# Attention's running maxima, its biases on ScalarE and its weight sums from a column of ones in a two-layer hybrid backbone

## The chip, the cores and the metric

One core of one Trainium2 chip runs the whole program. The metric is the device time of one execution in microseconds; the time before is 4437.48 us, the median of three runs (4432.41 to 4437.69). The kernel is written with a tile framework: it lays out the buffers, adds the semaphores, and orders each engine's instructions by priority with a timeline of its own at build time. On the chip each engine then works its queue in that fixed order.

## The reference

Two layers, each over 2048 latent tokens (which also read 512 cached context tokens) and 256 prompt tokens. One input projection feeds four parallel branches (latent attention, Hyena long convolution, S5 state space, chunked GLA); each is gated, and one output projection joins them. The change touches the attention alone:

```python
def one(qi):                                   # 128 queries, 4 heads
    s = jnp.einsum('bqhd,bkhd->bhqk', qi, k).astype(jnp.float32) * (MLA_QK ** -0.5)
    pr = jax.nn.softmax(s, axis=-1).astype(v.dtype)
    return jnp.einsum('bhqk,bkhd->bqhd', pr, v)
...
o_mla = block_attention(q, jnp.concatenate([k_ctx.astype(k.dtype), k], axis=1),
                        jnp.concatenate([v_ctx.astype(v.dtype), v], axis=1))
```

A latent query sees 512 + 2048 = 2560 keys, a prompt query 256. A head has 96 query and key columns and 64 value columns.

## The kernel before

Per layer there are 4 heads by 18 query tiles of 128 (16 latent, 2 prompt): 72 units, 144 in all. `mla_prep` (L307) projects queries, keys and values, splits each into an fp16 high part and an fp16 remainder, and stores them in DRAM; L415 and L416 write the value's two halves side by side, high part in columns 0 to 63 of `vd`. `load` in `attention` (L459) brings one head's keys and values into SBUF, two heads at a time (`bufs=2`).

A latent unit goes through three key chunks, of 1024, 1024 and 512. `scores` (L473) makes each chunk: for each part of 512 keys three matmuls into one PSUM bank (L485 to L487) and a maximum over it on VectorE (DVE, L488); for a chunk of two parts the larger of both (L492); the bias `nb`, which is minus the scaled maximum plus a constant (L493); then for each part the exponential on ScalarE (ACT, L495), which also gives the sum of the weights through `accum_out`, read by an instruction of its own that has the same line. `values` (L499) makes the fp16 high part of the weights on ACT, or in one of three cases on DVE (L508, L510), their remainder on POOL (L511), has both transposed by a DMA from SyncE's queue (L513), and multiplies with the values on TensorE (L517, L518) into one third of the bank `om`. Only one such bank exists, and the transposes that `emit` (L1951) makes share it. `combine` (L520) joins the three chunks: the smallest bias (L528), the chunks' factors (L529, ACT), the weighted sums and their reciprocal (L530 to L533), the three thirds of `om` with their factors (L536, L538) and the two halves of the columns (L540). The scores of the next chunk are issued before the values of this one, so `combine` comes after the first scores of the next unit.

The scores have three PSUM banks (`pss`), in the last part of layer 1 two more. The order around the attention is set by priority streams: GLA first, attention of heads 0 and 1 next, then Hyena, then attention of heads 2 and 3 with the output projection. These run interleaved, from about 1100 to 2440 us in layer 0 and from about 3330 us to the end in layer 1.

```python
mc = m[:, 2 * c:2 * c + 1]
if len(sps) > 1:
    nc.vector.tensor_tensor(out=mc, in0=mc, in1=m[:, 2 * c + 1:2 * c + 2], op=ALU.max)
nc.vector.tensor_scalar(out=nb[:, c:c + 1], in0=mc, scalar1=nssc, scalar2=LN2_15, op0=ALU.mult, op1=ALU.add)
for i, d in enumerate(sps):
    nc.scalar.activation(e[:, i * 512:min(i * 512 + 512, n)], d, AF.Exp, bias=nb[:, c:c + 1], scale=ssc,
                         accum_out=su[:, 2 * c + i:2 * c + i + 1])
```

Of the kernel before, what the change touches and what calls it, by code (L numbers as in the profile page):

```python
# [8 lines left out]
F32 = mybir.dt.float32  # L9
# [297 lines left out]
def mla_prep(s, l, p, tp, pp):  # L307
# [67 lines left out]
    for t in range(22):  # L375
# [39 lines left out]
        nc.scalar.activation(vd[:, :, 0:64], kv[:, :, 64:128], AF.Copy, scale=sv)  # L415
        nc.vector.scalar_tensor_tensor(out=vd[:, :, 64:128], in0=kv[:, :, 64:128], scalar=sv, in1=vd[:, :, 0:64],  # L416
# [38 lines left out]
def attention(s, l, units, tp, kp, bank, ps_o, emit):  # L455
# [3 lines left out]
    def load(h):  # L459

        out = []
        for a, b, nm in ((0, PAST + LAT, ""), (PAST + LAT, PAST + LAT + PR, "p")):
            K = kp.tile([128, 2, b - a], F16, tag="KT" + nm, name="KT" + nm)
            V = kp.tile([128, (b - a) // 128, 128], F16, tag="V" + nm, name="V" + nm)
            nc.sync.dma_start(K, s.KT[l][:, h, :, a:b])
            nc.sync.dma_start(V, s.V[l][h, :, a // 128:b // 128])
            out.append((K, V))
        return out
# [4 lines left out]
    def scores(u, c, k0, n):  # L473

        KT = u["KT"]
        e = tp.tile([128, 1024], F32, tag="e", name="e", bufs=3)[:, 0:n]
        nb, su, m = u["nb"], u["su"], u["m"]
        parts = range(0, n, 512)
        sps = []
        for i, a in enumerate(parts):  # L480
            w = min(512, n - a)
            d = bank(u["h"], u["t"])[:, 0:w]
            kh, kl = [KT[:, j, k0 + a:k0 + a + w] for j in range(2)]
            qh, ql = [u["qt"][:, j] for j in range(2)]
            nc.tensor.matmul(d, lhsT=qh, rhs=kh, start=True, stop=False)  # L485
            nc.tensor.matmul(d, lhsT=qh, rhs=kl, start=False, stop=False)  # L486
            nc.tensor.matmul(d, lhsT=ql, rhs=kh, start=False, stop=True)  # L487
            nc.vector.tensor_reduce(m[:, 2 * c + i:2 * c + i + 1], d, axis=AX.X, op=ALU.max)  # L488
            sps.append(d)
        mc = m[:, 2 * c:2 * c + 1]  # L490
        if len(sps) > 1:
            nc.vector.tensor_tensor(out=mc, in0=mc, in1=m[:, 2 * c + 1:2 * c + 2], op=ALU.max)  # L492
        nc.vector.tensor_scalar(out=nb[:, c:c + 1], in0=mc, scalar1=nssc, scalar2=LN2_15, op0=ALU.mult, op1=ALU.add)  # L493
        for i, d in enumerate(sps):
            nc.scalar.activation(e[:, i * 512:min(i * 512 + 512, n)], d, AF.Exp, bias=nb[:, c:c + 1], scale=ssc,  # L495
                                 accum_out=su[:, 2 * c + i:2 * c + i + 1])
        u["e"][c] = e

    def values(u, c, k0, n, first):  # L499

        e, V = u["e"].pop(c), u["V"]
        if first:
            u["om"] = ps_o.tile([128, 3, 128], F32, tag="om", name="om")
# [11 lines left out]
        for i in range(nk):  # L515
            v = V[:, k0 // 128 + i]
            nc.tensor.matmul(om[:, c], lhsT=pt[:, i], rhs=v, start=i == 0, stop=False)  # L517
            nc.tensor.matmul(om[:, c, 0:64], lhsT=pt[:, nk + i], rhs=v[:, 0:64], start=False, stop=i == nk - 1)  # L518

    def combine(u, C):  # L520
        nb, su, om = u["nb"], u["su"], u["om"]
        al, dn, mx = small(4, "al"), small(1, "dn"), small(1, "mx")
        w = tp.tile([128, 128], F32, tag="wo", name="wo")
        sc = su.rearrange("p (c i) -> p c i", i=2)
        last = C - 1
        if C > 1:

            nc.vector.tensor_reduce(mx, nb[:, 0:C], axis=AX.X, op=ALU.min)  # L528
            nc.scalar.activation(al[:, 0:C], nb[:, 0:C], AF.Exp, bias=mx, scale=-1.0)  # L529
            nc.vector.tensor_tensor(out=sc[:, 0:C], in0=sc[:, 0:C], in1=al[:, 0:C].unsqueeze(2).to_broadcast([128, C, 2]), op=ALU.mult)  # L530
            nc.vector.tensor_reduce(dn, su[:, 0:u["ns"]], axis=AX.X, op=ALU.add)
            nc.vector.reciprocal(dn, dn)
            nc.vector.tensor_scalar(out=al[:, 0:C], in0=al[:, 0:C], scalar1=dn, scalar2=None, op0=ALU.mult)  # L533
        else:
            nc.vector.reciprocal(al[:, 0:1], su[:, 0:1])
        nc.vector.tensor_scalar(out=w, in0=om[:, last], scalar1=al[:, last:C], scalar2=None, op0=ALU.mult)  # L536
        for c in range(last):
            nc.vector.scalar_tensor_tensor(out=w, in0=om[:, c], scalar=al[:, c:c + 1], in1=w, op0=ALU.mult, op1=ALU.add)  # L538
        o = pairs[u["h"] // 2, u["t"]][1]
        nc.vector.tensor_tensor(out=o[:, u["h"] % 2 * 64:u["h"] % 2 * 64 + 64], in0=w[:, 0:64], in1=w[:, 64:128], op=ALU.add)  # L540
# [16 lines left out]
    for h, t in units:  # L557
        if h not in kv:
            kv[h] = load(h)
        if (h // 2, t) not in pairs:  # L560
# [6 lines left out]
        u = dict(h=h, t=t, qt=pairs[h // 2, t][0][:, h % 2], KT=KT, V=V, e={}, m=small(8, "m"), nb=small(4, "nb"), su=small(8, "su"),  # L567
                 ns=5 if t < 16 else 1)
        if C > 1:
            nc.vector.memset(u["su"][:, 5:6], 0.0)  # L570
# [1264 lines left out]

PADF = 640


def body(tc, I, O, depth=DEPTH):
# [21 lines left out]
    with ExitStack() as top:  # L1861
# [5 lines left out]
        for l in range(depth):  # L1867
# [73 lines left out]
            kp = att.enter_context(pool(name=f"kv{l}", bufs=2, side="right"))  # L1941
            ps_s = att.enter_context(pool(name=f"pss{l}", bufs=3, space=PSUM))
# [89 lines left out]
```

## Time and profile before

| | |
|---|---|
| median of 3 runs | 4437.48 us |
| the profiled execution's own time | 4438.93 us |
| its span, first to last instruction | 4436.9 us |
| mean granted TensorE clock | 0.897 of full speed |
| TensorE matmul busy | 3680.0 us (83%) |
| VectorE (DVE) busy | 3222.7 us (73%) |
| ScalarE (ACT) busy | 2175.1 us (49%) |
| GpSimd (POOL) busy | 2048.8 us (46%) |
| DMA queue, share of 16 engines | 71.8% |

Busy time is a union of the instructions' spans. A view of stretches gives it for one stretch of the span; a view of lines gives groups of instructions by source line, with total, mean, and what ended the engine's idle time before them; a view of one line gives shortest, median and longest. The chain is followed back from the last instruction, at each step to what released it, so time on it is time that the end depended on; here it reaches back to about 3145 us.

### The profile page before, as it was taken

How to read it: one execution, taken by the hardware profiler on the slowest of the kernel's cores; microseconds unless marked ns; L12 is line 12 of the kernel's file. 1: busy time of each engine (PE TensorE's matmuls, PEld its weight loads, DVE VectorE, ACT ScalarE, POOL GpSimd, SP SyncE). 2: the span in 40 equal slices, each digit the busy share in tenths (PEclk: the TensorE clock that was granted, in tenths of full speed). 3: DMA queues.
4: the chain of work that ended last, by engine and by line, in shares of the span. 5: the costliest groups of instructions: out<-in, count | busy, mean ns of one | idle time of the engine just before them, and what ended most of it. 6: DMA issues, size and time to landing. Idle time of an engine off the chain costs nothing. (4 is left out here: it accounts for less than half of the span.)

```text
span 4436.9 us, 67211 instructions
## 1 busy us (share of the span) xinstructions
PE 3680.0 (83%) x21852; PEld 2141.3 (48%) x21852; DVE 3222.7 (73%) x8340; ACT 2175.1 (49%) x4333; POOL 2048.8 (46%) x2025
## 2 busy tenths in 40 slices
PE   6899889787877887769887688889998888667898
PEld 2644545343555555424443554545565555434444
DVE  4775589984788887776786678866548887767774
ACT  3533334556545564675453344363435555545563
POOL 2553354741555654654453244424325555434553
PEclk7999999898777887989998899999998888887999
DMA  7746657656776788998988565633448776999886
GB/s 207 193 122 182 175 146 191 188 155 221 168 172 150 173 186 212 239 235 203 250 192 203 148 156 145 154 111 123 145 156 193 184 168 157 210 246 240 173 185 157
DMA packets 1343430, 799.91 MB, mean 180 GB/s; under 512 B 989588, under 2 KB 1221296, under 8 KB 1341544
## 3 DMA queue, kind: packets, MB, share of 16 engines
q1 hardware_dynamic: 1343080, 795.63, 71.8%
q8 instruction: 173, 2.83, 0.3%
q14 instruction: 177, 1.45, 0.1%
HBM read 352.12 MB, written 207.37 MB: 126 GB/s over the span
## 5 line engine op out<-in xcount | busy, mean ns | idle before, releaser
L511 POOL TENSOR_TENSOR ph<-e,ph 128x1024 f16<-128x1024 f32 (+2 forms) x400 | 725.5, 1821 | 650.4 <-ACT ph L508 323.9
L495 ACT ACTIVATE e<-sp,nb,ssc 128x512 f32<-128x512 f32 (+1 forms) x656 | 499.9, 767 | 415.7 <-DVE nb L493 347.0
L488 DVE TENSOR_REDUCE m<-sp 128x1 f32<-128x512 f32 (+1 forms) x656 | 438.0, 676 | 172.0 <-PE sp L487 170.2
L268 PE MATMUL mm<-hT,ws 128*128 128x512 f16 (+1 forms) x1440 | 526.5, 366 | 26.2 <-DVE wqh L75 13.3
L269 PE MATMUL mm<-hT,ws 128*128 128x512 f16 (+1 forms) x1440 | 526.4, 366 | 0.0
L270 PE MATMUL mm<-hT,ws 128*128 128x512 f16 (+1 forms) x1440 | 525.8, 365 | 0.0
L517 PE MATMUL om<-V,pt 128*128 128x128 f16 x2560 | 303.8, 235 | 132.1 <-DMA pt<-ph 90.6
L485 PE MATMUL sp<-KT,qt 128*128 128x512 f16 x640 | 271.5, 424 | 102.5 <-ACT e L495 99.1
L517 PEld LDWEIGHTS <-pt 128*128 128x128 f16 x2592 | 258.9, 109 | 171.6 <-DMA pt<-ph 125.1
L508 ACT CAST ph<-e 128x1024 f16<-128x1024 f32 (+2 forms) x268 | 269.0, 1004 | 117.3 <-DMA pt<-ph 115.2
L518 PE MATMUL om<-V,pt 128*128 128x64 f16 x2560 | 293.7, 206 | 0.0
L518 PEld LDWEIGHTS <-pt 128*128 128x128 f16 x2592 | 248.2, 105 | 71.6 <-issue 58.5
L486 PE MATMUL sp<-KT,qt 128*128 128x512 f16 x640 | 271.4, 424 | 0.0
L487 PE MATMUL sp<-KT,qt 128*128 128x512 f16 x640 | 268.9, 420 | 0.0
L1606 PE MATMUL lv<-qh,kh 32*128 32x128 f32 x1440 | 227.7, 324 | 25.1 <-DVE m L492 10.2
L1606 PEld LDWEIGHTS lv<-qh,kh 32*128 32x128 f32 x1440 | 188.0, 218 | 98.8 <-issue 30.3
L1817 PE MATMUL mm<-wo,bh 128*128 128x512 f16 x576 | 223.7, 389 | 7.7 <-DVE oy L1820 6.7
L268 PE MATMUL mm<-ws,hT 128*128 128x256 f16 (+1 forms) x864 | 215.4, 264 | 15.8 <-ACT z L1688 13.4
L269 PEld LDWEIGHTS <-ws 128*128 128x128 f16 x1440 | 143.8, 100 | 175.2 <-issue 49.4
L1818 PE MATMUL mm<-wo,bh 128*128 128x512 f16 x576 | 224.1, 389 | 4.2 <-DVE wo L1772 4.2
L1819 PE MATMUL mm<-wo,bh 128*128 128x512 f16 x576 | 223.9, 389 | 2.8 <-DVE bh L1792 2.8
L268 PEld LDWEIGHTS <-ws 128*128 128x128 f16 x1440 | 143.9, 100 | 150.9 <-issue 26.1
(522 smaller groups left out, 9489.1 us busy)
## 6 DMA issues: line engine op xcount, KB each, us to landing
kab<-KS SPq DMA_DIRECT2D x128, 256.0 KB
wf<-in_w_in SPq DMA_DIRECT2D x22, 1024.0 KB
b<-br SPq DMA_DIRECT2D x36, 512.0 KB
A1F<-a SPq DMA_DIRECT2D x64, 256.0 KB
zg<-z SPq DMA_DIRECT2D x64, 256.0 KB
b<-A1F SPq DMA_DIRECT2D x32, 512.0 KB
KS<-k SPq DMA_DIRECT2D x64, 256.0 KB
aw<-in_ada_w SPq DMA_DIRECT2D x64, 256.0 KB
```

What stands on the lines that cost most here:

```text
L268: nc.tensor.matmul(ps, lhsT=lh, rhs=rh, start=i == 0, stop=False)
L269: nc.tensor.matmul(ps, lhsT=lh, rhs=rl, start=False, stop=False)
L270: nc.tensor.matmul(ps, lhsT=ll, rhs=rh, start=False, stop=i == n - 1)
L485: nc.tensor.matmul(d, lhsT=qh, rhs=kh, start=True, stop=False)
L486: nc.tensor.matmul(d, lhsT=qh, rhs=kl, start=False, stop=False)
L488: nc.vector.tensor_reduce(m[:, 2 * c + i:2 * c + i + 1], d, axis=AX.X, op=ALU.max)
L495: nc.scalar.activation(e[:, i * 512:min(i * 512 + 512, n)], d, AF.Exp, bias=nb[:, c:c + 1], scale=ssc, accum_out=su[:, 2 * c + i:2 * c + i ...
L508: nc.scalar.copy(ph[:, 0:n], e)
L511: nc.gpsimd.tensor_tensor(out=ph[:, n:2 * n], in0=e, in1=ph[:, 0:n], op=ALU.subtract)
L517: nc.tensor.matmul(om[:, c], lhsT=pt[:, i], rhs=v, start=i == 0, stop=False)
L518: nc.tensor.matmul(om[:, c, 0:64], lhsT=pt[:, nk + i], rhs=v[:, 0:64], start=False, stop=i == nk - 1)
L1606: nc.tensor.matmul(ps[:, cc], lhsT=kh[hh, cc], rhs=qh[hh, cc], start=True, stop=True, tile_position=(32 * h, 0))
```

## The change

Values: the two halves of the value columns change places, remainder first, high part in columns 64 to 127. A 129th column of ones is set in SBUF by POOL, so the tile's rows are 130 wide and the load fills 128 of them. The first value matmul takes 129 columns and the second takes 65 in place of 64, so that column 128 of `om` is the sum of the weights.

Scores: the maximum of a chunk is taken over all parts so far (one `tensor_reduce` per chunk), so it runs up; the bias is made on ACT; the exponentials no longer give sums.

Combine: the last chunk's factor is one, the other two come from the difference of biases; the first third of `om` is scaled on ACT, the second added on DVE with its factor, the third added on DVE; then the reciprocal of column 128, one half of the columns scaled on ACT, and the last instruction on DVE. The tiles `su`, `al`, `dn` and `mx` go. A pad of 192 bytes a partition is added.

```diff
-        nc.scalar.activation(vd[:, :, 0:64], kv[:, :, 64:128], AF.Copy, scale=sv)
-        nc.vector.scalar_tensor_tensor(out=vd[:, :, 64:128], in0=kv[:, :, 64:128], scalar=sv, in1=vd[:, :, 0:64],
+        nc.scalar.activation(vd[:, :, 64:128], kv[:, :, 64:128], AF.Copy, scale=sv)
+        nc.vector.scalar_tensor_tensor(out=vd[:, :, 0:64], in0=kv[:, :, 64:128], scalar=sv, in1=vd[:, :, 64:128],
...
-            V = kp.tile([128, (b - a) // 128, 128], F16, tag="V" + nm, name="V" + nm)
+            V = kp.tile([128, (b - a) // 128, 130], F16, tag="V" + nm, name="V" + nm)
             nc.sync.dma_start(K, s.KT[l][:, h, :, a:b])
-            nc.sync.dma_start(V, s.V[l][h, :, a // 128:b // 128])
+            nc.gpsimd.memset(V[:, :, 128:129], 1.0)
+            nc.sync.dma_start(V[:, :, 0:128], s.V[l][h, :, a // 128:b // 128])
...
-        mc = m[:, 2 * c:2 * c + 1]
-        if len(sps) > 1:
-            nc.vector.tensor_tensor(out=mc, in0=mc, in1=m[:, 2 * c + 1:2 * c + 2], op=ALU.max)
-        nc.vector.tensor_scalar(out=nb[:, c:c + 1], in0=mc, scalar1=nssc, scalar2=LN2_15, op0=ALU.mult, op1=ALU.add)
+        mc, k = m[:, 0:1], 2 * c + len(sps)
+        if k > 1:
+            mc = m[:, 5 + c:6 + c]
+            nc.vector.tensor_reduce(mc, m[:, 0:k], axis=AX.X, op=ALU.max)
+        nc.scalar.activation(nb[:, c:c + 1], mc, AF.Copy, scale=nssc, bias=LN2_15)
         for i, d in enumerate(sps):
-            nc.scalar.activation(e[:, i * 512:min(i * 512 + 512, n)], d, AF.Exp, bias=nb[:, c:c + 1], scale=ssc,
-                                 accum_out=su[:, 2 * c + i:2 * c + i + 1])
+            nc.scalar.activation(e[:, i * 512:min(i * 512 + 512, n)], d, AF.Exp, bias=nb[:, c:c + 1], scale=ssc)
...
-            nc.tensor.matmul(om[:, c], lhsT=pt[:, i], rhs=v, start=i == 0, stop=False)
-            nc.tensor.matmul(om[:, c, 0:64], lhsT=pt[:, nk + i], rhs=v[:, 0:64], start=False, stop=i == nk - 1)
+            nc.tensor.matmul(om[:, c], lhsT=pt[:, i], rhs=v[:, 0:129], start=i == 0, stop=False)
+            nc.tensor.matmul(om[:, c, 64:129], lhsT=pt[:, nk + i], rhs=v[:, 64:129], start=False, stop=i == nk - 1)
...
         if C > 1:
-            nc.vector.tensor_reduce(mx, nb[:, 0:C], axis=AX.X, op=ALU.min)
-            nc.scalar.activation(al[:, 0:C], nb[:, 0:C], AF.Exp, bias=mx, scale=-1.0)
-            nc.vector.tensor_tensor(out=sc[:, 0:C], in0=sc[:, 0:C], in1=al[:, 0:C].unsqueeze(2).to_broadcast([128, C, 2]), op=ALU.mult)
-            nc.vector.tensor_reduce(dn, su[:, 0:u["ns"]], axis=AX.X, op=ALU.add)
-            nc.vector.reciprocal(dn, dn)
-            nc.vector.tensor_scalar(out=al[:, 0:C], in0=al[:, 0:C], scalar1=dn, scalar2=None, op0=ALU.mult)
+            nc.scalar.activation(al, nb[:, 0:2], AF.Exp, bias=nb[:, 2:3], scale=-1.0)
+            nc.scalar.activation(w, om[:, 0], AF.Copy, scale=al[:, 0:1])
+            nc.vector.scalar_tensor_tensor(out=w, in0=om[:, 1], scalar=al[:, 1:2], in1=w, op0=ALU.mult, op1=ALU.add)
+            nc.vector.tensor_tensor(out=w, in0=om[:, 2], in1=w, op=ALU.add)
         else:
-            nc.vector.reciprocal(al[:, 0:1], su[:, 0:1])
-        nc.vector.tensor_scalar(out=w, in0=om[:, last], scalar1=al[:, last:C], scalar2=None, op0=ALU.mult)
-        for c in range(last):
-            nc.vector.scalar_tensor_tensor(out=w, in0=om[:, c], scalar=al[:, c:c + 1], in1=w, op0=ALU.mult, op1=ALU.add)
+            nc.scalar.copy(w, om[:, 0])
+        nc.vector.reciprocal(dn, w[:, 128:129])
+        nc.scalar.activation(w[:, 0:64], w[:, 0:64], AF.Copy, scale=dn)
         o = pairs[u["h"] // 2, u["t"]][1]
-        nc.vector.tensor_tensor(out=o[:, u["h"] % 2 * 64:u["h"] % 2 * 64 + 64], in0=w[:, 0:64], in1=w[:, 64:128], op=ALU.add)
+        nc.vector.scalar_tensor_tensor(out=o[:, u["h"] % 2 * 64:u["h"] % 2 * 64 + 64], in0=w[:, 64:128], scalar=dn, in1=w[:, 0:64],
+                                       op0=ALU.mult, op1=ALU.add)
```

## Rows read from the trace of the kernel before

**Rows 1.** Busy us (instructions) by stretch: PE, PEld, DVE, ACT, POOL; clock, DMA share, GB/s

```profile
1110.00:2442.00 1332.00, 1071.18 (x6559) 635.00 (x6558) 1032.94 (x2438) 719.50 (x1389) 695.89 (x516) 0.87 0.84 199
1776.00:1998.00 222.00, 160.21 (x892) 79.58 (x889) 171.77 (x345) 158.61 (x271) 126.25 (x82) 0.91 0.96 238
2109.00:2220.00 111.00, 92.89 (x495) 44.65 (x492) 78.49 (x192) 50.45 (x93) 45.65 (x25) 0.94 1.00 249
3330.00:4437.00 1107.00, 895.63 (x5916) 543.95 (x5915) 813.26 (x1967) 584.79 (x1171) 557.07 (x399) 0.87 0.83 191
3774.00:4107.00 333.00, 228.34 (x1439) 135.11 (x1437) 234.50 (x531) 178.78 (x350) 148.94 (x91) 0.82 0.96 232
```

**Rows 2.** The chain that ended last, by line, in the stretch 3330 to 4437 us

```profile
by line: DMA pt<-ph 12.7%; DVE m L488 6.9%; issue 6.0%; ACT e L495 4.7%; PE lv L1606 4.4%; DVE m L492 3.5%; SPq L513 3.2%; POOL ph L511 2.7%; PE om L517 2.5%; PE sp L485 2.4%; PE h L931 2.3%; PE h L936 2.2%; PE sp L486 2.0%; PE sp L487 1.9%
```

**Rows 3.** The same chain in order of time, around 3335 us: start, us, what

```profile
3334.02 1.34 DVE m L488 x2
3335.36 1.99 DVE m L492
3337.34 0.26 DVE nb L493 x2
...
3338.30 1.44 ACT e L495 x4
```

**Rows 4.** Waits between engines, whole span: us in total, times, longest us

```profile
ACT e L495 <- DVE nb L493: 347.0, 141, 9.2
...
PE sp L485 <- ACT e L495: 100.7, 77, 5.7
```

**Rows 5.** Groups by line, DVE: busy us, mean ns | idle us before, who ended it

```profile
L492 DVE TENSOR_TENSOR m<-m 128x1 f32<-128x1 f32 x256 | 129.0, 504 | 1.1
...
L538 DVE SCALAR_TENSOR_TENSOR wo<-om,al,wo 128x128 f32<-128x128 f32 x256 | 88.0, 344 | 2.3
...
L533 DVE TENSOR_SCALAR al<-al,dn 128x3 f32<-128x3 f32 x128 | 83.3, 651 | 1.2
...
L493 DVE TENSOR_SCALAR nb<-m,nssc 128x1 f32<-128x1 f32 x400 | 76.3, 205 | 2.1
...
L540 DVE TENSOR_TENSOR o<-wo 128x64 f32<-128x64 f32 x144 | 67.4, 468 | 1.3
...
L530 DVE TENSOR_TENSOR su<-su,al 128x6 f32<-128x6 f32 x128 | 62.1, 485 | 18.6 <-ACT e L495 14.7 <-ACT al L529 3.6
...
L536 DVE TENSOR_SCALAR wo<-om,al 128x128 f32<-128x128 f32 x144 | 49.3, 342 | 48.0 <-PE om L518 47.7
...
L532 DVE RECIPROCAL dn<-dn 128x1 f32<-128x1 f32 x128 | 19.8, 154 | 1.1
```

**Rows 6.** Lines L492 and L533, each by itself: shortest, median and longest ns

```profile
L492 DVE TENSOR_TENSOR m<-m x256: 136/157/2298, 1106.8 to 4345.2; 128x1 f32<-128x1 f32 x128
...
L533 DVE TENSOR_SCALAR al<-al,dn x128: 211/284/2195, 1124.9 to 4355.6; 128x3 f32<-128x3 f32 x128
```

**Rows 7.** Busy us of L488 alone on DVE, layer 1's attention stretch

```profile
3330.00:4437.00 1107.00, 217.53 (x325) 0.87 0.83 191
```

**Rows 8.** Busy us of L492 alone on DVE, the same stretch

```profile
3330.00:4437.00 1107.00, 68.28 (x128) 0.87 0.83 191
```

**Rows 9.** Groups by line and shape, ACT: busy us, mean ns | idle us before

```profile
L495 ACT ACTIVATION_READ_ACCUMULATOR e<-sp,nb,ssc 128x1 f32 x656 | 128.7, 196 | 0.0
...
L529 ACT ACTIVATE al<-nb,mx 128x3 f32<-128x3 f32 x128 | 37.7, 295 | 12.4 <-DVE mx L528 12.1
...
L1688 ACT ACTIVATE z<-mm,wun 128x128 f32<-128x128 f32 x36 | 13.1, 363 | 11.9 <-PE mm L270 11.8
```

**Rows 10.** Busy us of L495 alone on ACT, layer 1's attention stretch

```profile
3330.00:4437.00 1107.00, 264.00 (x656) 0.87 0.83 191
```

**Rows 11.** The DMA queue: packets, MB, share of 16 engines over the span

```profile
q1 hardware_dynamic: 1343080, 795.63, 71.8%
```

**Rows 12.** Groups by line, POOL: the nearest small memset

```profile
L1710 POOL MEMSET zc<- 128x1 f32 x24 | 2.3, 97 | 0.3 <-DMA zh<-zo 0.3
```

More of the change, by code (lines that the diff above doesn't have):

```diff
@@ L476, in scores @@
         e = tp.tile([128, 1024], F32, tag="e", name="e", bufs=3)[:, 0:n]
-        nb, su, m = u["nb"], u["su"], u["m"]
-        parts = range(0, n, 512)
+        nb, m = u["nb"], u["m"]
         sps = []
-        for i, a in enumerate(parts):
+        for i, a in enumerate(range(0, n, 512)):
             w = min(512, n - a)
@@ L502, in values @@
         if first:
-            u["om"] = ps_o.tile([128, 3, 128], F32, tag="om", name="om")
+            u["om"] = ps_o.tile([128, 3, 129], F32, tag="om", name="om")
         om = u["om"]
@@ L516, in values @@
             v = V[:, k0 // 128 + i]
-            nc.tensor.matmul(om[:, c], lhsT=pt[:, i], rhs=v, start=i == 0, stop=False)
-            nc.tensor.matmul(om[:, c, 0:64], lhsT=pt[:, nk + i], rhs=v[:, 0:64], start=False, stop=i == nk - 1)
+            nc.tensor.matmul(om[:, c], lhsT=pt[:, i], rhs=v[:, 0:129], start=i == 0, stop=False)
+            nc.tensor.matmul(om[:, c, 64:129], lhsT=pt[:, nk + i], rhs=v[:, 64:129], start=False, stop=i == nk - 1)
     def combine(u, C):
-        nb, su, om = u["nb"], u["su"], u["om"]
@@ L522, in combine @@
[L522 to L525, printed above, removed]
-        if C > 1:
-            nc.vector.tensor_reduce(mx, nb[:, 0:C], axis=AX.X, op=ALU.min)
-            nc.scalar.activation(al[:, 0:C], nb[:, 0:C], AF.Exp, bias=mx, scale=-1.0)
-            nc.vector.tensor_tensor(out=sc[:, 0:C], in0=sc[:, 0:C], in1=al[:, 0:C].unsqueeze(2).to_broadcast([128, C, 2]), op=ALU.mult)
-            nc.vector.tensor_reduce(dn, su[:, 0:u["ns"]], axis=AX.X, op=ALU.add)
-            nc.vector.reciprocal(dn, dn)
-            nc.vector.tensor_scalar(out=al[:, 0:C], in0=al[:, 0:C], scalar1=dn, scalar2=None, op0=ALU.mult)
-        else:
-            nc.vector.reciprocal(al[:, 0:1], su[:, 0:1])
@@ L536, in combine @@
-        nc.vector.tensor_scalar(out=w, in0=om[:, last], scalar1=al[:, last:C], scalar2=None, op0=ALU.mult)
-        for c in range(last):
-            nc.vector.scalar_tensor_tensor(out=w, in0=om[:, c], scalar=al[:, c:c + 1], in1=w, op0=ALU.mult, op1=ALU.add)
+        nb, om = u["nb"], u["om"]
+        al, dn = nb[:, 3:5], nb[:, 5:6]
+        w = tp.tile([128, 129], F32, tag="wo", name="wo")
+        if C > 1:
+            nc.scalar.activation(al, nb[:, 0:2], AF.Exp, bias=nb[:, 2:3], scale=-1.0)
+            nc.scalar.activation(w, om[:, 0], AF.Copy, scale=al[:, 0:1])
+            nc.vector.scalar_tensor_tensor(out=w, in0=om[:, 1], scalar=al[:, 1:2], in1=w, op0=ALU.mult, op1=ALU.add)
+            nc.vector.tensor_tensor(out=w, in0=om[:, 2], in1=w, op=ALU.add)
+        else:
+            nc.scalar.copy(w, om[:, 0])
@@ L566, in attention @@
         KT, V = kv[h][t >= 16]
[L567 to L570, printed above, removed]
+        u = dict(h=h, t=t, qt=pairs[h // 2, t][0][:, h % 2], KT=KT, V=V, e={}, m=small(8, "m"), nb=small(8, "nb"))
         for c, (k0, n) in enumerate(chunks):
@@ L1833, in outproj @@
             nc.sync.dma_start((O["y_sample"][0] if lat else O["y_prompt"][0])[o:o + 128], y)
+PADK = 48
 PADF = 640
@@ L1941, in body @@
             kp = att.enter_context(pool(name=f"kv{l}", bufs=2, side="right"))
+            kp.tile([128, PADK], F32, name="pad", bufs=1)
             ps_s = att.enter_context(pool(name=f"pss{l}", bufs=3, space=PSUM))
```

## The prediction

> **What bounds the kernel now.** I read the stretches first. The attention lies in two of them, 1332 + 1107 = 2439 us of the 4437 [rows 1]. There TensorE is busy 1071 + 896 = 1967 us (81%), VectorE (DVE) 1033 + 813 = 1846 us (76%), ScalarE (ACT) 1304 us (53%), and TensorE's clock is granted at 0.87 of full speed on average, between its levels of 1.2 and 2.4 GHz. No engine is full, so latency between engines counts. The chain comes next, because it says whose latency. It covers only layer 1's stretch, and the reader should see that attention makes it up: the transposes 12.7%, the maximum L488 6.9%, the exponential 4.7%, and L492, a maximum of two columns, 3.5% of 1107 us, which is 39 us for an instruction that has one element per partition to compute [rows 2]. In order of time one sees the loop: two maxima 1.34 us, L492 1.99 us, the bias, the exponentials [rows 3]. The waits say the same: ACT stood 347 us at the exponential for the bias, and TensorE stood 101 us for the exponentials to free a score bank [rows 4]. So DVE's small instructions sit in a loop that holds PSUM banks.
>
> **What goes on DVE.** The lines that go cost, in all, L492 129.0, L493 76.3, L530 62.1, L533 83.3, L536 49.3, L538 88.0, L540 67.4 us, and L528, L531 and L532, three alike, 3 x 19.8 = 59: together 615 us [rows 5]. A one-element memset per unit goes too and is left out.
>
> **What comes on DVE.** 3 x 128 = 384 reduces of a few columns at L532's 0.154 us: 59. Per latent unit one `scalar_tensor_tensor` and one `tensor_tensor` that read `om`, at 0.344 and 0.342 us: 88. 144 reciprocals at 0.154 us: 22. 144 final instructions with both inputs in SBUF, like L540, at its 0.468 us: 67. Together 236 us [rows 5], net 615 - 236 = **379 us less**. This rests on means that are far above the medians: L492 runs 136 to 2298 ns with median 157, L533 has median 284 against a mean of 651 [rows 5, 6]. With L492 and L533 at their medians (40 and 36 us) and L530, L540 and the new final instruction at 0.205 us, L493's mean (26, 30 and 30 us), 405 go and 199 come: net 206 us less. These are the two ends; I take the means, since an instruction that isn't there can't be stretched.
>
> **How much of that is on the path.** L488 has 0.069 x 1107 = 76 us on the chain of its 217.5 us busy, 35% [rows 2, 7]; L492 has 39 of 68.3, 57% [rows 2, 8]. I take the lower share for a mixed lot: 0.35 x 379 = 133 us, and assume that layer 0, which the chain doesn't reach but which runs the same instructions with DVE at 1033 of 1332 us, behaves alike. At 57% it is 216 us; from the medians at 35%, 72 us. Part of it is given back: in 222 + 111 + 333 = 666 us of the stretches the DMA engines are at 0.96 to 1.00 [rows 1], and there the transposes and Hyena's transfers are late next. That is 27%; 0.73 x 133 leaves **-97 us**.
>
> **ACT.** What goes is the accumulator read, 656 x 196 ns = 129 us. What comes is 400 biases at L529's 295 ns (118 us), 144 copies of a third of `om` at L1688's 363 ns (52 us) and 144 half-width scalings between those two, 0.33 us (48 us) [rows 9]: net +89 us. For the exponential 0.047 x 1107 = 52 of 264 us are on the chain, 20% [rows 2, 10]: **+18 us**, between 0 (ACT idles 1135 us in the stretches, which would cover it) and 31 at the 35% above. The bias is a multiply and an add: 205 ns on DVE [rows 5], about 295 on ACT [rows 9]. The Trainium skill (ScalarE: Activation LUTs, Rules for kernel authors) says to use VectorE, not ScalarE, for adding and multiplying. The trace agrees on the single instruction; taken as a rule for the sum it would charge 400 x 0.09 = 36 us more, but the engine that is charged has 1304 us of work where DVE has 1846 [rows 1].
>
> **Values.** A row of 130 columns makes the load land in pieces of 256 bytes: 128 x 20 = 2560 in place of 128. A packet cost 0.718 x 16 x 4437 / 1343080 = 0.038 us of one engine [rows 11], so a load takes some 2432 x 0.038 / 16 = 5.8 us more, and eight loads 46 us. That is the upper end; the lower is 0, because a load is asked for ahead of its head. I take the saturated share, 27%: **+12 us**. Sixteen memsets cost 0.1 us each [rows 12] and stand on POOL until an older head's buffer is free, with the subtractions L511 queued behind. No row shows that wait; four head changes at the mean wait of rows 4 (347 / 141 = 2.5 us) make 10 us, the lower end is nothing, and I take nothing, since the load waits for the same release. The extra matmul column is 1 in 128 of a line that has 2.5% of the chain [rows 2], under 0.3 us. Swapping the halves at L415 and L416 and the pad issue nothing different.
>
> **Sum.** -97 + 18 + 12 = -67 us. Against the profiled execution's 4438.9 us that is 4372; the median of the runs is 1.5 us below that execution, so **4370 us**. About 0.2% (9 us) is what a measurement can tell from no change.
>
> **Rival 1, slower: ACT's queue.** `combine` now puts ACT behind TensorE (the first third of `om`) and behind DVE (the reciprocal), 144 times each, and behind those waits stand the next chunk's bias and exponentials, which free the score banks. DVE's wait for `om` was 47.7 us at L536 [rows 5]; if every reciprocal costs ACT as long as a bias did, 144 x 2.46 = 354 us [rows 4], ACT idles 402 us more. At 20% to 35% on the path that is 80 to 141 us; at 27% it is 108, so 4370 + 108 = **4478 us**. It decides once more than 67 of those 402 us land on the path. For it: ACT obeys one order, fixed ahead. Against it: ACT has 1135 us to spare, and the three DVE instructions before the scaling take 0.84 us together.
>
> **Rival 2: DVE is the pace.** At L492's share and with nothing given back, -216 + 18 + 12 makes **4251 us**. For it: DVE at 78% in layer 0's stretch. Against it: TensorE at 81%.
>
> **Rival 3: the stall moves on.** The stretched instructions, L492, L530, L533 and L540, read SBUF alone, while L536 and L538, which read PSUM, have means near 0.34 us [rows 5]. If something on SBUF holds DVE until POOL is done, the next DVE instruction with such inputs takes over the rest of the stall, and only medians are saved: 0.73 x 72 = 53 us, and -53 + 30 makes **4414 us**. The Trainium skill (SBUF — State Buffer, Who interferes with whom) says that a VectorE instruction with two SBUF inputs contends with a GpSimd instruction that reads SBUF, and that the later one is blocked; the 136 to 2298 ns of L492 [rows 6] agree.
>
> **Rival 4: hidden, or not done.** If TensorE and the transposes set the pace everywhere, or if the bias on ACT makes DVE wait before it may write the next maximum in the same tile, the gain is gone: 4428 to 4446 us.
>
> **How the numbers follow.** The forecast has 0.47 (its own range 4310 to 4425), rival 2 0.15, rival 3 0.11, rival 4 0.09, rival 1 0.18. Faster by over 0.2%: 0.47 + 0.15 + 0.11 = 0.73; within: 0.09; slower: 0.18. A range of 4250 to 4465 leaves out half of rival 2 (0.07) and most of rival 1 (0.12).
>
> **What would show it.** Right: DVE busy in the two stretches falls by 200 to 380 us, no read of an accumulator is left, ACT's wait at the exponential falls well below 347 us, and L492's place on the chain is taken by a reduce near 0.15 us. Wrong: ACT's idle time ended by DVE's reciprocal or TensorE's `om` adds up to a hundred us or more (rival 1); other DVE lines grow in mean (rival 3); the chain is transposes and DMA throughout (rival 4).

## The result and the profile after

The changed kernel takes 4301.82 us (median of four runs, 4285.56 to 4310.24) against 4434.94 us for the kernel before in the same job: a ratio of 0.9708, 95% interval 0.9661 to 0.9754, 133 us faster. The forecast was 4370 us, 67 us faster; the measured time lies inside the range, on the forecast side, at twice the size. The profiled execution took 4304.43 us, its span is 4302.5 us and its mean granted clock 0.915.

The page's first part and its DMA part, of the kernel after:

```profile
span 4302.5 us, 66256 instructions
...
PE 3602.4 (84%) x21852; PEld 2093.6 (49%) x21852; DVE 3017.2 (70%) x7284; ACT 2284.6 (53%) x4367; POOL 2053.1 (48%) x2041
...
q1 hardware_dynamic: 1363560, 795.63, 74.5%
```

DVE's busy time fell from 3222.7 to 3017.2 us, by 205 us; ACT's rose by 110. TensorE has the same 21852 matmuls in 78 us less, and its mean clock rose from 0.897 to 0.915: 3680.0 x 0.897 and 3602.4 x 0.915 are both about 3300, so it is the same work at a higher granted clock.

To see where the 133 us lie, I cut each attention at its first score matmul, at the 161st of its 328 score parts, and at the end of its last exponential. A part is what one score bank holds: 512 keys, or 256 for a prompt query. Heads 0 and 1 have the first 164 parts, so the cut comes four parts before heads 2 and 3 begin; cut at the 165th part, the gains below are 77, 15, 44 and 16 us. The view of stretches with these cuts (columns as in rows 1), first the kernel before, then the one after; the order of the four rows is heads 0/1 and 2/3 in layer 0, then in layer 1:

```profile
1104.00:1715.00 611.00, 499.53 (x3343) 343.27 (x3342) 504.68 (x1170) 319.72 (x667) 346.23 (x305) 0.82 0.76 172
1715.00:2373.00 658.00, 521.21 (x3003) 268.49 (x3002) 497.91 (x1191) 386.49 (x707) 331.60 (x206) 0.92 0.90 220
3326.00:3872.00 546.00, 445.09 (x2958) 297.30 (x2958) 436.47 (x1053) 304.50 (x627) 300.66 (x244) 0.84 0.80 182
3872.00:4366.00 494.00, 392.92 (x2645) 219.06 (x2644) 353.61 (x866) 271.33 (x534) 241.32 (x143) 0.88 0.91 208
```

```profile
1109.00:1644.00 535.00, 447.22 (x3262) 308.62 (x3261) 441.66 (x896) 343.10 (x666) 348.13 (x304) 0.88 0.87 196
1644.00:2286.00 642.00, 530.96 (x3109) 278.91 (x3109) 456.61 (x946) 416.19 (x718) 337.65 (x212) 0.92 0.93 227
3251.00:3757.00 506.00, 410.02 (x2964) 277.00 (x2962) 377.75 (x799) 327.49 (x634) 305.39 (x247) 0.90 0.88 196
3757.00:4231.00 474.00, 375.00 (x2657) 207.59 (x2657) 313.57 (x593) 297.07 (x532) 238.75 (x145) 0.92 0.95 218
```

The reader is to see three things. The phases of heads 0 and 1 lost 76 and 40 us, those of heads 2 and 3 only 16 and 20. Where much was gained the clock rose most (0.82 to 0.88, 0.84 to 0.90) and the DMA share rose most (0.76 to 0.87, 0.80 to 0.88). Where little was gained the DMA engines already stood at 0.90 and 0.91. The rest of the program became some 18 us longer, in the pieces before, between and behind the two attentions.

A higher clock and a shorter loop cannot be told apart here. In the two phases of heads 0 and 1 TensorE's own busy time fell by 52 and 35 us and its idle time by only 24 and 5, so most of what was gained is the same matmuls at a higher granted clock. Among the runs below, too, the slower ones have the lower clock (0.898 in e3, 0.914 in e9). No run changes the clock alone, so whether the shorter waits raised it is argued, not shown.

The loop itself can be measured from the instruction records: the mean time from the first score matmul of a part to the end of its exponential, which is how long a score bank is held. In the order of the rows above it was 8.94, 8.63, 8.21 and 9.65 us; after, it is 8.05, 8.70, 7.36 and 9.94. It became 10% shorter where time was gained and no shorter where it was not. Times 160 parts over 611 or 535 us, 2.3 to 2.4 of the three banks are held at any time in the phases of heads 0 and 1, before and after, so there the phase and the holding time shrank together; which of the two drove the other this product cannot tell.

DVE's lines in the kernel after (columns as in rows 5):

```profile
L489 DVE TENSOR_REDUCE m<-sp 128x1 f32<-128x512 f32 (+1 forms) x656 | 435.6, 676 | 153.8 <-PE sp L488 152.9
...
L511 DVE CAST ph<-e 128x512 f16<-128x512 f32 (+1 forms) x132 | 131.4, 995 | 75.8 <-ACT e L497 36.0 <-DMA pt<-ph 33.5 <-ACT xs L885 3.5
L536 DVE SCALAR_TENSOR_TENSOR o<-wo,nb 128x64 f32<-128x64 f32 x144 | 111.4, 774 | 67.4 <-ACT wo L534 67.0
...
L494 DVE TENSOR_REDUCE m<-m 128x1 f32<-128x2 f32 (+2 forms) x384 | 54.1, 147 | 1.6
```

and one line by itself, the running maximum (shortest, median and longest in ns after the count):

```profile
L494 DVE TENSOR_REDUCE m<-m x384: 94/146/182, 1111.8 to 4203.0; 128x1 f32<-128x2 f32 x64, 128x1 f32<-128x5 f32 x64, 128x1 f32<-128x4 f32 x64
```

L492 of before, a `tensor_tensor` of two columns, ran up to 2298 ns [rows 6]; the reduce that replaces it never passed 182 ns. But the stall is not gone. The cast L511, which the change does not touch, has a mean of 995 ns. It was L510 in the kernel before, whose view of lines has for it

```profile
L510 DVE CAST ph<-e 128x512 f16<-128x512 f32 (+1 forms) x132 | 87.4, 662 | 75.7 <-DMA pt<-ph 47.3 <-ACT e L495 25.1 <-POOL ph L511 1.6
```

and so 662 ns; the final instruction L536 has 774 ns where its like had 468 [rows 5].

The waits that answer to rows 4, kernel after (who waited for whom: us, times, longest):

```profile
ACT nb L495 <- DVE m L494: 279.7, 153, 8.1
...
PE sp L486 <- ACT e L497: 76.7, 67, 10.1
```

ACT's wait in the loop, at the bias now, went from 347 to 280 us, TensorE's for a free score bank from 101 to 77. The chain of waits reaches back only to about 3905 us in this execution, so its shares are not comparable with rows 2; L494 has 2 us on it. Runs with a longer chain follow below.

### The profile page after: what moved, and what is told of

Same layout as the page of the kernel before. It is cut to its first block, busy times and chain, and to the rows that moved or that the text cites. A ratio compares the mean times of both kernels' runs of the same rounds, so it can differ in the third digit from the quotient of the medians.

```text
span 4302.5 us, 66256 instructions
## 1 busy us (share of the span) xinstructions
PE 3602.4 (84%) x21852; PEld 2093.6 (49%) x21852; DVE 3017.2 (70%) x7284; ACT 2284.6 (53%) x4367; POOL 2053.1 (48%) x2041
## 3 DMA queue, kind: packets, MB, share of 16 engines
q1 hardware_dynamic: 1363560, 795.63, 74.5%
## 5 line engine op out<-in xcount | busy, mean ns | idle before, releaser
L497 ACT ACTIVATE e<-sp,nb,ssc 128x512 f32<-128x512 f32 (+1 forms) x656 | 473.0, 768 | 21.6 <-POOL ph L512 11.8
L518 PE MATMUL om<-V,pt 128*128 128x129 f16 x2560 | 299.3, 232 | 132.5 <-DMA pt<-ph 101.8
L486 PE MATMUL sp<-KT,qt 128*128 128x512 f16 x640 | 264.1, 413 | 79.0 <-ACT e L497 74.1
L519 PE MATMUL om<-V,pt 128*128 128x65 f16 x2560 | 289.2, 202 | 0.0
L495 ACT ACTIVATE nb<-m,nssc 128x1 f32<-128x1 f32 x400 | 111.8, 291 | 287.3 <-DVE m L494 279.7
L487 PE MATMUL sp<-KT,qt 128*128 128x512 f16 x640 | 264.2, 413 | 0.0
L488 PE MATMUL sp<-KT,qt 128*128 128x512 f16 x640 | 262.7, 410 | 0.0
L269 PEld LDWEIGHTS <-ws 128*128 128x128 f16 x1440 | 144.0, 100 | 192.2 <-issue 65.3
L268 PEld LDWEIGHTS <-ws 128*128 128x128 f16 x1440 | 144.4, 100 | 151.5 <-issue 25.1
L270 PEld LDWEIGHTS <-ws 128*128 128x128 f16 x1440 | 143.7, 100 | 151.7 <-issue 25.8
```

The lines of the kernel that those rows point to most:

```text
L268: nc.tensor.matmul(ps, lhsT=lh, rhs=rh, start=i == 0, stop=False)
L269: nc.tensor.matmul(ps, lhsT=lh, rhs=rl, start=False, stop=False)
L270: nc.tensor.matmul(ps, lhsT=ll, rhs=rh, start=False, stop=i == n - 1)
L518: nc.tensor.matmul(om[:, c], lhsT=pt[:, i], rhs=v[:, 0:129], start=i == 0, stop=False)
L519: nc.tensor.matmul(om[:, c, 64:129], lhsT=pt[:, nk + i], rhs=v[:, 64:129], start=False, stop=i == nk - 1)
```

## The experiments

Every ratio is to the kernel before in the same job, with its 95% interval; a difference of ratios is given in points, 1 point being 0.01, some 44 us. The change was measured in one job, e1 to e4 in a second, e5 to e8 in a third and e9 to e12 in a fourth.

**How far a small edit of the plan moves the time.** One case in three of the weights' cast goes to DVE; starting that count one later moves which ones. The edit was made to the kernel before (e4_null) and to the one after (e8_null_after).

```diff
-    turn = [0]
+    turn = [1]
```

> The kernel before with the same work: the count that sends every third fp16 copy of the weights to DVE starts one later, so other chunks' copies go there, and the plan is made anew around them. If plans of the same work differ little, 4435 us within 15. Theory C (another plan by luck) needs 40 us or more of difference, either way.

> The changed kernel with the same work and the count of the fp16 copies one later, as was done to the kernel before, where it cost 24 us. It tells how far two plans of the same work lie apart here: within 25 us of 4302 us if the gain belongs to the work; if the gain is a lucky plan, this one loses half of it or more, 4365 us or above.

Before: 4452.72 us, 1.0054 [1.0033, 1.0075]. After: 4323.67 us, 0.9788 [0.9764, 0.9812], which is 22 us and 0.8 points above the change. The edit is not the null edit that it was meant to be. A latent unit has three chunks, so every third cast is always the same chunk: DVE had the chunk of 512 keys and now gets one of 1024. The line of the cast in e4:

```profile
L510 DVE CAST ph<-e x132: 282/694/2716, 1116.7 to 4370.2; 128x1024 f16<-128x1024 f32 x128, 128x256 f16<-128x256 f32 x4
```

Its median was 427 ns before, and ACT's busy time fell by 44 us in each of the two. So 0.5% and 0.8% are what taking some 44 us of casting off ACT and the new order around it do together. The one run that gives every engine the change's instructions in the change's shapes is e11 below; it lies 0.55 points above the change, measured in another job, and the two intervals overlap. Single runs of one plan spread as far, those of the change from 4285.56 to 4310.24 us. In what follows "the other plans" are e8 to e11, which all do the change's useful work. A step of less than their distance from the change, 0.8 points, says nothing, and one of 1 point is suggestive only.

**The two halves of the change.** e1_scores is the kernel before with the running maximum and ACT's bias only; e2_sums is that kernel with the column of ones, no sums from the exponential and the new joining, but with one maximum per chunk, the bias on DVE, the smallest bias and a factor for every third.

e1_scores:

```diff
-            nc.vector.tensor_tensor(out=mc, in0=mc, in1=m[:, 2 * c + 1:2 * c + 2], op=ALU.max)
-        nc.vector.tensor_scalar(out=nb[:, c:c + 1], in0=mc, scalar1=nssc, scalar2=LN2_15, op0=ALU.mult, op1=ALU.add)
+            nc.vector.tensor_reduce(mc, m[:, 0:k], axis=AX.X, op=ALU.max)
+        nc.scalar.activation(nb[:, c:c + 1], mc, AF.Copy, scale=nssc, bias=LN2_15)
```

e2_sums, against the kernel after:

```diff
-            nc.scalar.activation(al, nb[:, 0:2], AF.Exp, bias=nb[:, 2:3], scale=-1.0)
+            nc.vector.tensor_reduce(mx, nb[:, 0:C], axis=AX.X, op=ALU.min)
+            nc.scalar.activation(al, nb[:, 0:C], AF.Exp, bias=mx, scale=-1.0)
...
-            nc.vector.tensor_tensor(out=w, in0=om[:, 2], in1=w, op=ALU.add)
+            nc.vector.scalar_tensor_tensor(out=w, in0=om[:, 2], scalar=al[:, 2:3], in1=w, op0=ALU.mult, op1=ALU.add)
```

> The scores' half of the change alone on the kernel before: running maxima by one reduce per chunk and the bias on ACT; the sums by the accumulator, their read and the old combine stay. Theory A (DVE's load): time falls in proportion to DVE's busy time; L492 and L493 go (205 us), 384 reduces come (57 us), net -148 of the -340 us that the lines of the whole change make, so about 0.43 of the 133 us: 4377 us. Theory B (the loop that holds the score banks): what counts lies between a chunk's maximum and its exponential, which is all in this half: 100 us or more of the 133, so 4335 us or less. Theory C (another plan by luck): any time between 4380 and 4470, unrelated to either.

> The other half alone: column of ones, no accumulator, combine with two steps on ACT; each chunk's own maximum and the bias on DVE stay, and so does the smallest bias, so the last third of the output gets its factor. DVE loses about 410 us of lines and gets 230 us. Theory A: net -180 us by lines, 0.55 of the gain: 4362 us. Theory B: combine is off the loop that holds the score banks, so 30 us or less: 4405 us or more. Theory D (ACT's queue): the two waits of combine on ACT cost what DVE saves: 4435 us or more, with ACT's idle time ended by the reciprocal at 100 us or more.

e1: 4356.01 us, 0.9851 [0.9825, 0.9876], between what its theories A and B expect. e2: 4418.95 us, 0.9973 [0.9951, 0.9994], as theory B has it. The scores are the larger half; the sums alone are hardly more than nothing. DVE's busy time does not tell the halves apart, as the first parts of their pages show, e1 and then e2:

```profile
PE 3621.5 (83%) x21852; PEld 2108.8 (48%) x21852; DVE 3140.7 (72%) x8068; ACT 2271.5 (52%) x4735; POOL 2051.8 (47%) x2025
```

```profile
PE 3667.2 (83%) x21852; PEld 2135.3 (48%) x21852; DVE 3128.3 (71%) x7684; ACT 2199.8 (50%) x3965; POOL 2056.8 (47%) x2041
```

The scores took 82 us off DVE and gained 1.5 points; the sums took 94 us off it and gained 0.3. The chain shows the difference. In e2, which keeps L492 (as L493), over layer 1's attention, 3298 to 4360 us:

```profile
by line: DMA pt<-ph 14.4%; DVE m L489 6.9%; issue 5.6%; ACT e L496 4.7%; PE lv L1600 4.3%; DVE m L493 3.8%; PE sp L486 3.0%; DVE ph L510 2.8%; ACT ph L508 2.7%; SPq L513 2.6%; PE sp L487 2.5%; PE sp L488 2.5%; PE h L930 2.4%; PE om L517 2.3
```

Of 1062 us that is 40 us for L493, as L492 had 39 before [rows 2]. The running maximum that replaces it has 3 to 6 us on the layer 1 part of the chain in e1, e3, e8, e9, e10 and e11 (worked out from the same records). The two halves together would make 0.9851 x 0.9973 = 0.9824; the change has 0.9708, and the other plans have 0.976 to 0.979. So half or more of the missing 1.2 points may be the plan or the job; what is left, 0.4 to 0.6, may be that the halves help each other, and the runs do not separate these.

**The bias back on DVE** (e3_bias_dve is the kernel after with this edit):

```diff
-        nc.scalar.activation(nb[:, c:c + 1], mc, AF.Copy, scale=nssc, bias=LN2_15)
+        nc.vector.tensor_scalar(out=nb[:, c:c + 1], in0=mc, scalar1=nssc, scalar2=LN2_15, op0=ALU.mult, op1=ALU.add)
```

> The changed kernel with one undo: the bias is made on DVE again (400 instructions of 0.2 us there, 400 of 0.29 us fewer on ACT). Theory A: DVE gets 78 us back, at the 0.65 us of time per us of DVE busy that the change showed 51 us: 4353 us. Theory B: the loop gets shorter by 0.09 us a chunk on the instruction but waits for DVE's queue a second time: between 4290 and 4330 us. The rule that adding and multiplying belong on VectorE: faster than the change, 4290 us or less.

4376.36 us, 0.9874 [0.984, 0.9908], slower than all three expectations: 1.7 points of the 2.9 are gone, 0.9 to 1.1 against the other plans. It is also e2 with the running maximum in L492's place (and so without the smallest bias and the last third's factor): that is worth 1.0 point.

**DVE or ACT loaded with dead work, in a new tile.** e5_dve_load makes each bias a second time on DVE, for nobody; e6_accum brings the exponentials' sums back, for nobody. Both write to a new small tile of four buffers, to each of which the framework gives 32 bytes: 128 bytes a partition.

```diff
+        nc.vector.tensor_scalar(out=small(1, "xx"), in0=mc, scalar1=nssc, scalar2=LN2_15, op0=ALU.mult, op1=ALU.add)
```

```diff
+            nc.scalar.activation(e[:, i * 512:min(i * 512 + 512, n)], d, AF.Exp, bias=nb[:, c:c + 1], scale=ssc,
+                                 accum_out=su[:, 2 * c + i:2 * c + i + 1])
```

> The changed kernel with a dead instruction: 400 times DVE makes the bias a second time, into a tile that nobody reads, in the place and form in which it was made before; the loop goes through ACT as in the change. Undoing the bias alone had cost 73 us. Theory A (what DVE's queue holds sets the pace): most of that is back, 4350 us or more. Theory B (what counts is that the bias is one instruction ahead of the exponential in ACT's own queue, and DVE is passed once): 4302 us within 15.

> The changed kernel with the sums of the exponentials taken by the accumulator as well, into a tile that nobody reads: 656 reads of 0.196 us are back on ACT (129 us), DVE as in the change. If ACT's time were free, as 1135 us of idle in the stretches suggested, 4302 us within 15. At the 20% of the path that the prediction gave ACT, 26 us: 4328 us. If ACT now is the engine that the loop runs through, the full overlap-free share, 60 us or more: 4360 us or more.

e5: 4749.23 us, 1.0747 [1.0725, 1.077]. e6: 4787.11 us, 1.083 [1.0804, 1.0856]. Both lie hundreds of us beyond what was expected (the open bounds of 4350 and 4360 us or more hold only in the letter), and alike though the loads are on different engines. The view of stretches of e5, for the GLA's matmuls L1601 alone (us of PE, PEld, then clock, DMA share, GB/s):

```profile
1082.00:2059.00 977.00, 71.59 (x408) 60.05 (x408) 0.81 0.87 194
2059.00:2500.00 441.00, 61.75 (x312) 57.08 (x312) 0.81 0.44 138
...
3411.00:4050.00 639.00, 0.00 (x0) 0.00 (x0) 0.86 0.99 221
4050.00:4450.00 400.00, 140.24 (x720) 129.77 (x720) 0.56 0.24 72
```

In layer 1 not one of GLA's 720 matmuls runs before 4050 us. By then 229 of the attention's 328 parts have been through; none begins between 4032 and 4417 us, where GLA runs, with the DMA engines at 0.24 and the clock granted at 0.56, and its last 99 parts come after. In layer 0, 312 of GLA's 720 come behind the attention. In e6 GLA runs in the same places. The two kernels thus measured another order of the branches, not a load.

**The same dead work in columns that were spare** (e9_dead_bias, e10_dead_sums: `nb` has eight columns, six are used):

```diff
+        nc.vector.tensor_scalar(out=nb[:, 6:7], in0=mc, scalar1=nssc, scalar2=LN2_15, op0=ALU.mult, op1=ALU.add)
```

```diff
+                                 accum_out=nb[:, 6 + i:7 + i])
```

> The dead bias again, now into a spare column of a tile that is there anyway, so that the attention takes no byte more of SBUF than in the change. Theory E (what cost 450 us in e5 and e6 was their footprint, which drove GLA out from beside the attention): GLA runs beside heads 0 and 1 again and the time is below 4400 us. Then, of the bias: Theory A (what DVE's queue holds sets the pace): 50 to 70 us above the change, 4350 to 4375 us. Theory B (DVE is passed once in the loop): 4302 us within 30, the spread of two plans of the same work seen so far.

> The sums by the accumulator again, into spare columns of a tile that is there anyway. Theory E: below 4400 us. Of ACT: if its time is free, 4302 us within 30; at the prediction's 20% of 129 us, 4328 us; if every microsecond of ACT counts as one of DVE did (0.65), 84 us: 4386 us.

e9: 4331.09 us, 0.9766 [0.9733, 0.9799]. e10: 4330.19 us, 0.9765 [0.9726, 0.9803]. Both lie 28 to 29 us above the change and within 1 us of e11, which adds nothing and ran in the same job. The added work is there. The line of e9's dead bias:

```profile
L496 DVE TENSOR_SCALAR nb<-m,nssc 128x1 f32<-128x1 f32 x400 | 82.5, 207 | 4.2
```

and e10's dead reads of the accumulator:

```profile
L497 ACT ACTIVATION_READ_ACCUMULATOR e<-sp,nb,ssc 128x1 f32 x656 | 128.0, 195 | 0.0
```

82 us on DVE and 128 us on ACT, both inside the attention, cost no more than another plan does (the engines' busy time rose by 40 and 58 us). Against e11 that is 0.03 points with an uncertainty of half a point, or some 20 us: a price of 0.65 us per us of DVE is excluded, one of 0.26 hardly. The nearest comparison for the bias is e9 with e3, here their pages' first parts, e9 and then e3:

```profile
PE 3612.3 (83%) x21852; PEld 2100.5 (48%) x21852; DVE 3056.9 (71%) x7684; ACT 2287.6 (53%) x4365; POOL 2057.9 (47%) x2041
```

```profile
PE 3646.5 (83%) x21852; PEld 2128.5 (49%) x21852; DVE 2996.2 (68%) x7684; ACT 2200.3 (50%) x3967; POOL 2060.3 (47%) x2041
```

Both have DVE's bias 400 times. In e9 nobody reads it and ACT makes its own; in e3 the exponentials wait for it. e9 has 61 us more on DVE and 87 more on ACT, and is 1.1 points faster: the intervals do not overlap, though the distance is little more than that between two plans. It suggests that an instruction costs by who waits for it and not by running. But the bias's own time on the chain does not show it: in layer 1 it has 5 us in e3 and 9 to 11 on ACT in e8 to e11.

**No pad** (e11_no_pad):

```diff
-            kp.tile([128, PADK], F32, name="pad", bufs=1)
```

> The changed kernel without the pad, 192 bytes a partition less than before and after the change. If only too much footprint hurts, 4302 us within 30. If addresses as such decide which buffers wait for which, a difference of 40 us or more in either direction.

4330.14 us, 0.9763 [0.9728, 0.9799]: within the spread of plans.

**ACT's part of the joining back on DVE** (e7_comb_dve):

```diff
-            nc.scalar.activation(w, om[:, 0], AF.Copy, scale=al[:, 0:1])
+            nc.vector.tensor_scalar(out=w, in0=om[:, 0], scalar1=al[:, 0:1], scalar2=None, op0=ALU.mult)
...
-        nc.scalar.activation(w[:, 0:64], w[:, 0:64], AF.Copy, scale=dn)
+        nc.vector.tensor_scalar(out=w[:, 0:64], in0=w[:, 0:64], scalar1=dn, scalar2=None, op0=ALU.mult)
```

> The changed kernel with both of combine's steps on ACT (the scaled copy of the first third, the scaling of one half) put back on DVE: DVE gets 128 x 0.34, 16 x 0.3 and 144 x 0.2 us, some 78 us, and ACT no longer waits there for TensorE and for the reciprocal (37 + 16 + 33 us in the changed kernel). Theory A: 50 us slower, 4352 us. Rival of the prediction (ACT's queue pays for these waits): 20 us or more faster, 4280 us or less.

4349.2 us, 0.9849 [0.9825, 0.9873]: 1.4 points above the change, 0.6 to 0.9 above the other plans, which is hardly beyond their spread. Theory A's 4352 us met the number, but its price, 0.65 us per us of DVE, did not hold in e9. What is left is the place of these steps behind `om`, or one more plan; that is open.

**The stretched last instruction, read from PSUM** (e12_half_psum): the scaled half goes into the bank `om`, so that L536's like has one input in PSUM.

```diff
-        nc.scalar.activation(w[:, 0:64], w[:, 0:64], AF.Copy, scale=dn)
+        lo = om[:, 0, 0:64]
+        nc.scalar.activation(lo, w[:, 0:64], AF.Copy, scale=dn)
```

> The changed kernel with the scaled half of the columns put by ACT into the output bank (its first third has been read by then), so that the last instruction of combine reads one input from PSUM and one from SBUF. If two inputs from SBUF are what stretches DVE's instructions to 2 us while POOL works, its mean falls from 0.77 to 0.35 us or less and none is longer than 0.5 us: 60 us less on DVE, at 0.65 some 40 us: 4262 us. Against it: the one output bank is held longer, by the reciprocal, ACT's scaling and the last instruction, about 1 us a unit or more: 4302 us to 4340 us if that is on the path.

4403.88 us, 0.9924 [0.9891, 0.9957], above both expectations. The line itself did what was hoped (ns, shortest, median, longest):

```profile
L537 DVE SCALAR_TENSOR_TENSOR o<-wo,nb,om x144: 259/273/283, 1152.5 to 4329.0; 128x64 f32<-128x64 f32 x144
```

against the same instruction in the kernel after, with both inputs in SBUF:

```profile
L536 DVE SCALAR_TENSOR_TENSOR o<-wo,nb x144: 261/420/2154, 1154.5 to 4252.6; 128x64 f32<-128x64 f32 x144
```

144 x (774 - 274) ns = 72 us went from that line, and the kernel lost 1.4 to 2.2 points against the change and the other plans. The one bank `om` is now busy until the last instruction has read it: from a unit's last value matmul to the next unit's first, the mean over the units of a layer by the instruction records went from 8.1 to 10.4 us (8.4 and 7.7 in e8 and e11), and ACT's wait for `om` at its first step rose from 36.8 to 68.6 us. That this longer hold is the whole of the loss is argued, not shown.

**The holding time of a score bank in the other runs.** Measured as above in the phases of heads 0 and 1 (8.94 and 8.21 us before, 8.05 and 7.36 after), it is 8.78 and 8.15 us in e2, 8.31 and 7.74 in e1, 8.50 and 7.71 in e3, 8.47 and 7.37 in e9, 7.9 to 8.05 and 7.4 in e8, e10 and e11. It sorts the halves as the times do. Two runs warn against taking it as the whole story: e9 holds its banks as long as e3 in layer 0, and e12 has 7.53 and 7.42 and is slow all the same, because its phases of heads 2 and 3 became longer (671 and 515 us against 642 and 474).

No version tried here beats the change.

## Why the prediction was right, and where its sum was wrong

**The signs.** In the four phases DVE's busy time fell from 1793 to 1590 us, ACT's wait in the loop from 347 to 280, and no read of an accumulator is left at the exponential, as foretold. L492's place on the chain went to a reduce of 0.15 us, as e11's chain shows. Other DVE lines grew in mean, which was rival 3's sign. ACT's wait is a poor sign: it is 366 us in e1, which gained 1.5 points, and 288 in e2, which gained 0.3.

**The direction and the plans.** Five plans with the change's useful work (the change, e8, e9, e10, e11) lie between 0.9708 and 0.9788, at 4302 to 4331 us. So 93 to 104 us is what four of the five gain in their own jobs, and some 30 to 40 of the 133 us may be the particular plan or the job. The forecast of -67 is short of both. The 0.2% that the prediction took for what can be told from no change was too little: the four runs of the kernel before lie between 4409.48 and 4437.69 us.

**The step that failed: what of DVE's time is on the path.** The prediction took 379 us off DVE, the end by means, as one mixed lot at one price, 0.26 in all. Measured: 205 us off DVE and 133 us off the time, 0.65 of it. Both factors were off, in opposite directions, so that the product of -97 came close to the typical plan's gain by luck.

The first factor was too large. DVE's busy time fell by 205 us here, and by 222 and 241 in e10 and e11, which give DVE the same instructions. That looks like the medians' 206, but it is another measure: busy time is a union, and the spans of neighbouring instructions overlap in the records. Added up by line, as the prediction's 379 was, DVE lost 268 us here, 289 in e10 and 317 in e11, between its two ends. "An instruction that isn't there can't be stretched" is true and beside the point, since a part of the stall falls on others: L511 went from 662 to 995 ns, the last instruction to 774, and the DVE lines that the change does not touch, L511 among them, grew by 87 us together.

The second factor was wrong in kind, because the lot is not mixed. The scores' half took 82 us off DVE for 1.5 points and the sums' half 94 us for 0.3, and e9 adds 82 us off the loop for nothing measurable; so 0.65 is no price for the next kernel either. What had a price was a place in the loop that holds the score banks. L492 had 39 us on the chain in layer 1 [rows 2], and the running maximum has 3 to 6; if layer 0 is alike, that is some 69 us. e2 to e3, which makes that replacement, gained 1.0 point, 43 us. The bias, 76 us of DVE at 205 ns each [rows 5], gained 0.9 to 1.7 points, 38 to 74 us, when it went to ACT (e3 against the other plans and the change). Each of these two by itself is only a little beyond the distance between two plans; together, e2 against the five, they are 1.9 to 2.7 points and well beyond it. Why the bias at 291 ns on ACT is better than at 207 ns on DVE is not settled by a run: ACT's wait in the loop is 237 us in e3 and 280 in the change, and the bias's time on the chain is no shorter on ACT, so neither of these is what became shorter.

**What is given back to the DMA engines.** Right in direction: the phases of heads 2 and 3, half of the attention's time, gave 36 us of 152, and there the bank's holding time did not fall at all. In e8 to e11, cut in the same way, heads 0 and 1 gained 80 to 127 us and heads 2 and 3 from -2 to 38. The phases of heads 0 and 1 gained 116 of 1157 us, 10%; at that rate the others would have gained 115 of 1152, and 79 of the 231 us, a third, were given back, against the 27% assumed. That the DMA engines took them rests on their share alone; no run eases the transfers. With that share now at 0.87 to 0.95 in all four phases, the next such gain is likely to be smaller.

**ACT: +18 us, not to be told from 0.** e10 puts 128 us of accumulator reads back and lies within 1 us of e11. That speaks for the lower end, zero, but the uncertainty of some 20 us would hide 18. The rule of the Trainium skill (ScalarE: Activation LUTs, Rules for kernel authors), to add and multiply on VectorE, agrees here with the single instruction (207 ns on DVE in e9, 291 ns on ACT). It would have led the wrong way: e3, which follows it, is slower than the change and, by 0.9 points or more, than every other plan.

**Values: +12 us.** The packets came as counted, 1363560 - 1343080 = 20480, which is 8 x 2432 for the latent values as worked out, and 8 x 128 for the two pieces of the prompt's loads, which the prediction left out. Their time rose from 0.718 x 4436.9 = 3186 to 0.745 x 4302.5 = 3205 us of 16 engines, 20 us where 46 was the upper end. What of it reached the end was not tried apart. The pad (e11) costs nothing that shows; the ones and the wider matmul were not tried apart, but the whole half with them (e2) was 0.3 points faster.

**The rivals.** Rival 1, ACT's queue, was to cost ACT 402 us of idle time. The waits of the kernel after say 36.8 us for `om` at L528, another 16 at L532 and 33.2 for the reciprocal at L534: 86 us in all instead of 402, too little for the 67 on the path from which it decides unless nearly all of it lay there, and the time fell. Rival 2, DVE as the pace, does not fit e1 and e2, which took alike from DVE and gained 1.5 and 0.3 points. Rival 3, the stall that moves on, was right that part of it does (268 us by line, between its 206 and 379) and wrong about the end, 4414 us. The heirs L511 and L536 are not what an exponential waits for, though they stay in DVE's queue: on layer 1's chain L511 has 32 us in e11 where its like had 16 before, and L536 has 16 where its like had 13, which is less than the 34 us that L492 gave up. The rule it cited (Trainium skill, SBUF — State Buffer, Who interferes with whom) held in e12: with one input in PSUM no instance passed 283 ns, with two in SBUF the longest took 2154. The cast L511 reads one input and was stretched up to 2365 ns as well, so two inputs are not the only case. Rival 4, hidden or not done, fell with the result.

## What to carry to other kernels

Price an instruction by the loop in which it stands and by who waits for it there, not by its engine's busy time; a dead copy of it in spare space, with nobody waiting, helps to tell the two apart. Measure first what a small edit of the order does, because here such edits did 0.5% to 0.8% and half of the steps that one would like to explain are no larger; check by instructions and shapes per engine that the edit moved no work, and run the change again in the same job as its ablations. Keep the buffers the same size in such tests, or they measure a different order of the whole program.

## What was not expected

**128 bytes.** A small tile of 128 bytes a partition cost 435 and 472 us (e5, e6 against their spare-column twins e9 and e10 by ratio: 1.0747 - 0.9766 and 1.083 - 0.9765, times 4430). In e5 the phases of heads 0 and 1 became shorter, 394 and 396 us against 535 and 506, with no GLA beside them, and then in layer 1 GLA ran while the attention stood still. Removing 192 bytes (e11) did nothing that shows. That the tile takes the room that GLA's buffers had beside the attention's is the likely reason, but no run shows where the limit lies.

**Stalls are inherited in part.** Taking 1056 instructions off DVE (8340 to 7284) saved less than their means say and more than their medians. The untouched cast, in the same shapes, has a mean of 770 to 995 ns in the change and in e1, e2, e3, e7 and e9 to e12, which all leave the cast's count alone, against 662 before, with its median in the change still at 429 against 427. e12 removed 72 us of a stall by another input, and DVE's busy time fell by as much, from 3017 to 2938 us. So part of the stall passes on when an instruction vanishes, and in e12, one case, none did when the instruction no longer read both inputs from SBUF.
